# S5 queues re-ordered, and the weights behind each norm converted in a room of their own without GpSimd

## The chip, the core and the metric

The kernel runs on one core of a Trainium2 chip. The engines named here are TensorE (PE), VectorE (DVE), ScalarE (ACT), GpSimd (POOL) and SyncE (SP), each with an instruction queue that it works off in order; DMA transfers are issued from SP's and ACT's queues. The metric is the device time of one execution in microseconds, the median of the runs.

## The reference

One step of a trunk with two layers. Layer 0 mixes with an S5 state space model, layer 1 with an RG-LRU; each is followed by a residual layer norm, a gated FFN with a causal convolution of width 3, and another norm. There are 512 prompt tokens with 16 meta tokens ahead (528 positions) and 8 running sequences of 8 tokens, 592 columns in all; the model is 1024 wide, the FFN 2816.

```python
def _trunk(h, ...):
    for i in range(DEPTH):                       # DEPTH = 2
        if i % N_MIXERS == 0:
            mix, sr, si = s5_mixer(h, ...)       # u = x @ w_in; B u; scan; C s + d u; gelu; GLU @ w_out
        else:
            mix, hr, cb = rglru_mixer(h, ...)    # conv4, gates, linear recurrence, @ w_out
        h = layer_norm(DN_ALPHA * h + mix, ...)
        f, fb = conv_ffn(h, ...)                 # up, conv3, gelu(gate) * value, down
        h = layer_norm(DN_ALPHA * h + f, ...)

def layer_norm(x, g, b):
    mu = jnp.mean(x, -1, keepdims=True)
    var = jnp.mean(jnp.square(x - mu), -1, keepdims=True)
    return (x - mu) * lax.rsqrt(var + LN_EPS) * g + b
```

All of it is computed in float32, and the states and convolution histories are returned with the outputs.

## The kernel before

**Layout and products.** Activations lie transposed: 128 channels on the partitions, the 592 columns along them, eight tiles `RES[0..7]` for the 1024 channels. A product is made in two halves of 296 columns. Each float32 operand is held as a rounded high part and the remainder, and every block of 128 x 128 weights costs three matmuls, in `mm3`:

```python
T.matmul(out, hi[:, k, :], xh, start=start, stop=False)    # L151, hi,whi
T.matmul(out, hi[:, k, :], xl, start=False, stop=False)    # L152, lo,whi
T.matmul(out, lo[:, k, :], xh, start=False, stop=stop)     # L153, hi,wlo
```

**Weights.** `load` fetches a 512 KB tile by SP's queue into one of three raw buffers; `convert_hi` (L122, ACT) makes `whi`, `convert_lo` (L131, DVE, or POOL where the call passes `G`) makes `wlo = raw - whi`, each from a pool of four. `weights` hands the next pair out, in a fixed order of `keys`, and normally converts ahead as it does so.

**Stages.** By the trace: S5 until 204 us, its GLU until about 297, norm 0 until 336, FFN 0 until 741, norm 1 until 779, RG-LRU until 939, norm 2 until 969, FFN 1 until 1372, the last norm and the output until 1401.

**S5.** The order of the work is written by hand (`manual_schedule`): each engine's queue holds its instructions in the order in which the Python calls stand. Ahead of the loop, a generator `ahead` of small operations on the parameters is pumped by `some(n)`, while `split_x` (L295 the low half) and the first projections run. `turn` transposes operators through PSUM (L504, copied at L506), `turn_b` does so for the B operators that `bbar` makes (L414 to L416), `phases` and `tables` (L462 to L479) make the discretised coefficients, `projection(m, h)` multiplies by `w_in` and `projected` copies the result out (L449).

The loop has eight steps s. A step spreads the B operators by a matmul with a selection (`flip_b` L519, `flipped` L525 and L526, giving `bt`; `spread` and `operators` L534 to L542, giving `xw`), makes the state inputs (`states`, L605, 64 matmuls of 74 columns), scans on DVE (`scans`, L618 to L626), turns the states back (`turned`, L634 to L639, giving `sx`), saves the `ends` of the states (L643, L644 on ACT, which read `sx`), and makes the outputs of the step before (`outputs`, L656 from `sx`, L660 from the Toeplitz operator `toe`). `lags`, `windows` and `assemble` (L559, L562, L550 on POOL, L569, L584) build those operators. `gy_hi` and `gy_lo` (L685, L689) split the gelu's output for the GLU, whose first products stand at the end of step 6.

**Norms.** `skewed` overlaps a norm with the last products ahead of it (`tail` of them) and with the first products behind it. Columns 0 to 295 are finished for all tiles first; while the norm works on them, PE makes the other half. A norm sums z and z squared on POOL (L906, L907), totals them over channels by a matmul with ones (L920, L922), makes mean and scale (`centered`, L934 to L955, POOL L940), and applies them tile by tile (`applied`: DVE L973, ACT L974 the high part, DVE L979 the low part). `plan` is a table that says what else is queued at which tile: numbers are the evacuations of tail products, functions are weight conversions. The three first weights behind the norm, `nxt`, are handed out without converting ahead; the plan converts them, seven of the nine low parts in all on POOL.

**FFN.** A pool of its own opens with the FFN; it loads the convolution's history by ACT's queue and scales it on POOL (`hist`, L1138 to L1141). The norm's offsets are added to `RES` by POOL (L1002) at the start; L1161 adds the history and L1166 is the gelu.

## Time and profile before

| | |
|---|---|
| runs | 1402.67, 1402.8, 1412.2 us; median 1402.8 |
| profiled execution | 1403.13 us; span 1401.3 us, mean granted TensorE clock 0.980 |
| PE busy | 1333.1 us (95%) in 10680 matmuls |
| DVE busy | 840.2 us (60%) |
| ACT busy | 582.7 us (42%) |
| POOL busy | 301.1 us (21%) |
| chain that ended last | PE 76%, DVE 17%, ACT 4%, issue 2%, POOL 1% |
| weight conversions on DVE, L131 | 181, mean 1265 ns |

The span is the time from the first to the last instruction on the profiled execution. PE is the engine with the most work, so the places of interest are those where it is not busy: the page's slices show them in the first seventh of the span and in short dips after it. "PEclk" is the clock that TensorE was granted, as a share of 2.4 GHz; the lower of its two levels, 1.2 GHz, reads 0.5. A matmul that waits shows in brackets how long and for which instruction of which engine.

### The profile page before, as it was taken

How to read it: one execution, taken by the hardware profiler on the slowest of the kernel's cores; microseconds unless marked ns; L12 is line 12 of the kernel's file. 1: busy time of each engine (PE TensorE's matmuls, PEld its weight loads, DVE VectorE, ACT ScalarE, POOL GpSimd, SP SyncE). 2: the span in 40 equal slices, each digit the busy share in tenths (PEclk: the TensorE clock that was granted, in tenths of full speed). 3: DMA queues.
4: the chain of work that ended last, by engine and by line, in shares of the span. 5: the costliest groups of instructions: out<-in, count | busy, mean ns of one | idle time of the engine just before them, and what ended most of it. 6: DMA issues, size and time to landing. Idle time of an engine off the chain costs nothing.

```text
span 1401.3 us, 25545 instructions
## 1 busy us (share of the span) xinstructions
PE 1333.1 (95%) x10680; PEld 1308.4 (93%) x10680; DVE 840.2 (60%) x1421; ACT 582.7 (42%) x942; POOL 301.1 (21%) x368
## 2 busy tenths in 40 slices
PE   6979889999999999999998999998999999999995
PEld 6978889988999999999998999998999999999994
DVE  8758936358655255535547889849655245535546
ACT  3645534235343133313433587734444124313433
POOL 1313402247000000000037431167100000000036
PEclk9979979999999999999999999999999999999998
DMA  6525554211322222222221212221322222222211
GB/s 221 162 82 138 132 177 136 76 61 61 106 76 84 83 76 85 67 91 91 66 82 61 93 45 92 96 68 61 107 90 77 90 78 85 74 97 81 77 52 68
DMA packets 72035, 127.65 MB, mean 91 GB/s; under 512 B 21232, under 2 KB 43888, under 8 KB 71920
## 3 DMA queue, kind: packets, MB, share of 16 engines
q1 hardware_dynamic: 62160, 120.45, 27.1%
q10 hardware_dynamic: 9760, 5.57, 1.4%
q8 instruction: 84, 1.38, 0.4%
q14 instruction: 31, 0.25, 0.1%
HBM read 113.35 MB, written 12.66 MB: 90 GB/s over the span
## 4 chain that ended last, share of the span: by engine, by line
PE 76%; DVE 17%; ACT 4%; issue 2%; POOL 1%; DMA 0%; SPq 0%; DVEq 0%; ACTq 0%
PE mm L152 24%; PE mm L153 24%; PE mm L151 24%; DVE wlo L131 2%; DVE res L973 1%; DVE lo L979 1%; PE mm L656 1%; DVE xw L542 1%; DVE res L945 1%; PE mm L660 1%; PE mm L605 1%; DVE t L635 1%; ACT res L479 1%; DVE res L968 1%; ACT whi L122 1%
## 5 line engine op out<-in xcount | busy, mean ns | idle before, releaser
L152 PE MATMUL mm<-lo,whi 128*128 128x296 f32 (+2 forms) x2816 | 843.9, 300 | 17.9 <-DVE lo L979 9.8
L151 PE MATMUL mm<-hi,whi 128*128 128x296 f32 (+2 forms) x2816 | 845.4, 300 | 13.8 <-ACT whi L122 6.8
L153 PE MATMUL mm<-hi,wlo 128*128 128x296 f32 (+2 forms) x2816 | 842.7, 299 | 2.8 <-DVE wlo L131 2.8
L152 PEld LDWEIGHTS mm<-lo,whi 128*128 128x128 f32 x2816 | 535.2, 190 | 23.9 <-DVE lo L979 14.5
L151 PEld LDWEIGHTS mm<-hi,whi 128*128 128x128 f32 x2816 | 535.1, 190 | 16.5 <-ACT whi L122 6.8
L153 PEld LDWEIGHTS mm<-hi,wlo 128*128 128x128 f32 x2816 | 534.7, 190 | 4.0 <-DVE wlo L131 4.0
L131 DVE TENSOR_TENSOR wlo<-wraw,whi 128x1024 fp32r<-128x1024 f32 (+1 forms) x181 | 228.2, 1265 | 220.0 <-ACT whi L122 219.3
L122 ACT ACTIVATE whi<-wraw 128x1024 fp32r<-128x1024 f32 (+1 forms) x188 | 194.5, 1039 | 302.5 <-PE mm L152 297.5
L1161 POOL TENSOR_TENSOR tmp<-tmp,hist 128x16 f32<-128x16 f32 x88 | 20.5, 235 | 697.4 <-DVE tmp L1158 697.4
L1156 DVE SCALAR_TENSOR_TENSOR tmp<-mm,sm,tmp 128x512 f32<-128x512 f32 (+2 forms) x176 | 132.1, 750 | 0.0
L1160 ACT ACTIVATE stg<-mm 128x18 f32<-128x18 f32 x88 | 16.4, 186 | 185.6 <-DVE tmp L1158 185.5
L1208 DVE TENSOR_TENSOR res<-mm,res 128x296 f32<-128x296 f32 (+3 forms) x48 | 26.0, 558 | 80.5 <-PE mm L153 80.5
L1151 ACT ACTIVATE tmp<-mm,sm 128x592 f32<-128x592 f32 (+1 forms) x88 | 72.2, 822 | 0.0
L1167 DVE TENSOR_TENSOR tmp<-tmp 128x592 f32<-128x592 f32 (+1 forms) x44 | 33.8, 767 | 38.7 <-ACT tmp L1166 38.7
L906 POOL TENSOR_TENSOR s<-s,res 128x296 f32<-128x296 f32 (+2 forms) x45 | 41.8, 930 | 60.9 <-DVE res L1114 31.2
L168 DVE TENSOR_TENSOR lo<-tmp,hi 128x592 fp32r<-128x592 f32 (+2 forms) x48 | 36.7, 764 | 29.6 <-ACT hi L167 29.6
L550 POOL TENSOR_TENSOR v<-cq,ap 128x512 f32<-128x512 f32 x32 | 42.5, 1359 | 49.8 <-ACT cq L494 41.1
L167 ACT ACTIVATE hi<-tmp 128x592 fp32r<-128x592 f32 (+2 forms) x48 | 33.1, 690 | 43.9 <-DVE tmp L1167 30.0
L1002 POOL TENSOR_SCALAR res<-res,sm 128x592 f32<-128x592 f32 (+1 forms) x24 | 49.2, 2065 | 6.3 <-DVE lo L979 6.3
L907 POOL TENSOR_TENSOR s<-s,tmp 128x296 f32<-128x296 f32 (+2 forms) x53 | 50.4, 955 | 0.2 <-ACT tmp L902 0.2
L902 ACT ACTIVATE tmp<-res 128x296 f32<-128x296 f32 (+2 forms) x56 | 24.0, 445 | 58.0 <-DVE res L1208 24.7
L1206 DVE SCALAR_TENSOR_TENSOR res<-res,mm 128x592 f32<-128x592 f32 (+1 forms) x16 | 12.2, 762 | 59.2 <-PE mm L153 59.2
(277 smaller groups left out, 1237.4 us busy)
## 6 DMA issues: line engine op xcount, KB each, us to landing
wraw<-in_wup SPq DMA_DIRECT2D x88, 512.0 KB, 3.4
wraw<-in_wdn SPq DMA_DIRECT2D x32, 448.0 KB, 3.3
wraw<-in_w5o SPq DMA_DIRECT2D x16, 512.0 KB, 4.3
wraw<-in_wdn SPq DMA_DIRECT2D x16, 512.0 KB, 3.5
wraw<-in_wri SPq DMA_DIRECT2D x16, 512.0 KB, 3.6
wraw<-in_w5i SPq DMA_DIRECT2D x8, 512.0 KB, 4.4
td<-lagsb SPq DMA_DIRECT2D x8, 512.0 KB, 3.4
lagged<-td SPq DMA_DIRECT2D x8, 512.0 KB, 4.2
```

Source lines behind the costliest of these rows:

```text
L122: A.activation(hi[:, 0:kk, :], t[:, 0:kk, :], AF.Copy)
L131: eng.tensor_tensor(lo[:, 0:kk, :], t[:, 0:kk, :], hi[:, 0:kk, :].bitcast(F32), op=ALU.subtract)
L151: T.matmul(out, hi[:, k, :], xh, start=start, stop=False)
L152: T.matmul(out, hi[:, k, :], xl, start=False, stop=False)
L153: T.matmul(out, lo[:, k, :], xh, start=False, stop=stop)
L168: V.tensor_tensor(lo[:, scols], src[:, scols], hi[:, scols].bitcast(F32), op=ALU.subtract)
L550: G.tensor_tensor(v[:, m], c[:, a, :, :, None].to_broadcast(sh), b[:, NQ * q:NQ * q + NQ, None, 1:CH + 1].to_broadcast(sh), op=ALU.mult)
L906: G.tensor_tensor(self.s1[:, cs_], RES[0][:, cs_] if m == 1 else self.s1[:, cs_], z, op=ALU.add)
L907: G.tensor_tensor(self.s2[:, cs_], self.s2[:, cs_], sq[:, cs_], op=ALU.add)
L1002: G.tensor_scalar(z, z, bm, None, op0=ALU.add)
L1151: A.activation(acc[:, d0:NT], X(d0, NT), AF.Identity, scale=w[2], bias=fcb[:, l, m:m + 1])
L1156: V.scalar_tensor_tensor(acc[:, a:TP], X(a - sh, TP - sh), w[k], acc[:, a:TP], op0=ALU.mult, op1=ALU.add)
```

## The change

Two parts that have nothing to do with each other, and one small move.

*S5's order.* The opening makes 9 and then 6 of the small parameter operations ahead of the first low half of the weights, where it made 24 and one per tile; `projected(1, 1)` comes ahead of the rest of them; the turn of B operators 0 and 1 comes behind `project(3, 0)`, in another PSUM tile. `bbar(5, 8)`, `phases(1)` and `tables(1)` move from step 0 to ahead of the loop. In each step from 2 on, `flipped(s + 1)` comes ahead of `ends(s - 1)`. `projection(7, 0)` and `toeplitz(0)` move from step 1 to the end of step 0. In steps 6 and 7, `gy_lo(s - 3)` comes ahead of `turned(s)`.

*Weights behind a norm.* Where `nxt` is given, `skewed` opens a pool with two buffers each for `whi` and `wlo`. The first two weights behind the norm are converted into it, on ACT and DVE, one behind each of the last two evacuations of the first half. The third is converted in the plan: its high part at "late", its low part behind the last tile of the first half. No conversion behind a norm is done on POOL. The pool closes with the norm, and the FFN's pool opens after it.

*Room.* The RG-LRU's pool is closed ahead of the tiles of norm 2 instead of behind that norm.

```diff
+        def room(i, name):
+            if i in beside:
+                return beside[i].tile([P, 8, P], F32R, tag=f"x{name}", name=name, bufs=2)
+            return wp.tile([P, 8, P], F32R, tag=name, name=name, bufs=4)
...
-                some(24)
+                some(9)
                 for k in range(DM):
                     split_x(k, 0)
                     if k == 0:
                         load(1)
+                        some(6)
                         convert_next()
-                    some(1)
-                    if k == 3:
-                        load(2)
+                    else:
+                        some(1)
+                load(2)
...
+                projected(1, 1)
                 some(200)
-                projected(1, 1)
...
-                turn_b(0, 2)
                 convert_next()
                 project(3, 0)
+                turn_b(0, 2, 1)
+                projected(3, 0)
                 flip_b(0)
-                projected(3, 0)
...
                 bbar(2, 5)
-                assemble(1)
+                phases(1)
+                bbar(5, 8)
                 flip_b(1)
                 flipped(1)
+                assemble(1)
...
                 projection(4, 0)
+                tables(1)
                 turn_b(2, 5)
...
                 for s in range(DM):
                     last = s == DM - 1
+                    if 1 < s < DM - 1:
+                        flipped(s + 1)
                     run(ends, s - 1)
...
-                    if 1 < s < DM - 1:
-                        flipped(s + 1)
...
-                    run(toeplitz, s - 1)
+                    if s > 1:
+                        toeplitz(s - 1)
...
-                    if s == 1:
-                        projection(7, 0)
                     run(outputs, s - 1)
                     run(fetch_gy, s - 2)
+                    if s >= DM - 2:
+                        gy_lo(s - 3)
                     turned(s)
...
                         flipped(2)
-                        phases(1)
-                        tables(1)
                         convert_next()
                         projection(6, 0)
-                        bbar(5, 8)
+                        turn_b(5, 8)
                         phases(2)
                         tables(2)
                         projection(6, 1)
-                        turn_b(5, 8)
                         phases(3)
                         tables(3)
-                    run(gy_lo, s - 3)
+                        projection(7, 0)
+                        toeplitz(0)
+                    if s < DM - 2:
+                        run(gy_lo, s - 3)
...
-            with tc.manual_schedule():
+            with ExitStack() as ex:
+                if nxt:
+                    own = ex.enter_context(tc.tile_pool(name=f"own{norm.i}", bufs=1))
+                    beside.update({keys.index(key): own for key in nxt[:2]})
+                ex.enter_context(tc.manual_schedule())
                 for i, m in enumerate(end):
                     pair(i, 0)
                     prod(m, 0, 0, n, ahead=i < tail // 2)
                     evac(m, 0)
+                    if nxt and i >= tail - 2:
+                        load(at["conv"] + 3)
+                        convert(at["conv"] + 1)
...
-                        {"late": lambda: (A.activation(scr, scr, AF.Tanh), convert_hi(at["conv"] + 2)),
-                         0: [lambda: convert_lo(at["hi"], G)], 1: [0], 3: [1],
-                         5: [lambda: convert(at["conv"] + 1, G)]}, tail=2)
+                        {"late": lambda: (A.activation(scr, scr, AF.Tanh), convert_hi(at["conv"] + 1)),
+                         1: [0], 3: [1], 8: [lambda: convert_lo(at["hi"])]}, tail=2)
...
-        PLAN = {"late": lambda: convert_hi(at["conv"] + 2),
-                0: [lambda: convert_lo(at["conv"] + 1, G), 1, lambda: convert_lo(at["conv"] + 1)],
-                3: [2], 4: [3], 6: [lambda: convert(at["conv"] + 1, G)]}
+        PLAN = {"late": lambda: convert_hi(at["conv"] + 1), 0: [1], 3: [2], 4: [3],
+                8: [lambda: convert_lo(at["hi"])]}
...
+        rgs.close()
         HL3 = hltiles()
         opened = skewed(list(range(3, DM)), ro_prod, ro_evac, norm, gcols, HL3, up_first(1), DM, (4, 6), PLAN, slots)
         nc.sync.dma_start(o_rgc, rgc)
         nc.sync.dma_start(o_rgh, rgh)
-        rgs.close()
```

The lines of the changed kernel stand a few numbers lower: L504 becomes L509, L605 L610, L656 L661, L689 L694, L131 L136, L973 L983, L979 L989, L1208 L1225.

PE's queue in steps 0 and 1, before. L504 turns B operators 5 to 7, L605 is `states(1)`, L656 and L660 are `outputs(0)`; at the dots stand the 24 products of projection (7,0).

```order
L504 MATMUL mm<-ident,bb 128x128 x3
L605 MATMUL mm<-u,xw 64x74 x32
L559 MATMUL mm<-cq,bst_123 32x16 x8
L562 MATMUL mm<-v,bst_123 32x112 x16
L534 MATMUL mm<-aT,sel_126 128x128 x8
...
L656 MATMUL mm<-sx_154,v 128x74 x32
L660 MATMUL mm<-u,toe 128x74 x8
```

The same place with the change; at the dots stand the products of projections (6,1) and (7,0), 48 of them.

```order
L509 MATMUL mm<-ident,bb 128x128 x3
...
L610 MATMUL mm<-u,xw 64x74 x32
L564 MATMUL mm<-cq,bst_123 32x16 x8
L567 MATMUL mm<-v,bst_123 32x112 x16
L539 MATMUL mm<-aT,sel_126 128x128 x8
L661 MATMUL mm<-sx_154,v 128x74 x32
L665 MATMUL mm<-u,toe 128x74 x8
```

The turn comes 24 products earlier, and `outputs(0)` stands directly behind the operators' matmuls (L534, now L539), with projection (7,0) ahead of all of them.

DVE's queue at the end of step 6, before. L626 is the scan, L542 the operators of the next step, L634 to L639 `turned`, L689 `gy_lo(3)`.

```order
L626 SCALAR_TENSOR_TENSOR t<-d_1938,t 128x296 x2
L570 SCALAR_TENSOR_TENSOR lagsb<-diag,sp_107,mm 128x16
L542 TENSOR_TENSOR xw<-bt,mm 128x1024 x2
L634 TENSOR_TENSOR t<-t,res_73 128x592
L635 TENSOR_TENSOR t<-t,res_73 128x592
L638 TENSOR_TENSOR sx_154<-t 128x4x74
L639 TENSOR_TENSOR sx_154<-t 128x4x74
L689 TENSOR_TENSOR lo<-res_70,hi 128x592
L570 SCALAR_TENSOR_TENSOR lagsb<-diag,sp_107,mm 128x16
```

With the change:

```order
L631 SCALAR_TENSOR_TENSOR t<-d_1938,t 128x296 x2
L575 SCALAR_TENSOR_TENSOR lagsb<-diag,sp_107,mm 128x16
L547 TENSOR_TENSOR xw<-bt,mm 128x1024 x2
L694 TENSOR_TENSOR lo<-res_70,hi 128x592
L639 TENSOR_TENSOR t<-t,res_73 128x592
L640 TENSOR_TENSOR t<-t,res_73 128x592
L643 TENSOR_TENSOR sx_154<-t 128x4x74
L644 TENSOR_TENSOR sx_154<-t 128x4x74
L575 SCALAR_TENSOR_TENSOR lagsb<-diag,sp_107,mm 128x16
```

`gy_lo` stands ahead of the four instructions of `turned`, which come one instruction later.

DVE's queue in norm 1, before. L1208 is an evacuation of the FFN's down products, L951 to L955 are the statistics of the first half, L973 applies tile 0 and tile 1; the second weight's low part stands between them.

```order
L951 TENSOR_TENSOR tmp<-tmp 128x296
L945 TENSOR_TENSOR res_69<-res_69,mm 128x296
L953 SCALAR_TENSOR_TENSOR tmp<-tmp 128x296
L945 TENSOR_TENSOR res_70<-res_70,mm 128x296
L955 SCALAR_TENSOR_TENSOR tmp<-tmp 128x296
L973 SCALAR_TENSOR_TENSOR res_67<-res_67,sm,tmp 128x296
L1208 TENSOR_TENSOR res_72<-mm,res_72 128x296
L131 TENSOR_TENSOR wlo<-wraw,whi 128x1024
L973 SCALAR_TENSOR_TENSOR res_68<-res_68,sm,tmp 128x296
L979 SCALAR_TENSOR_TENSOR lo<-res_67,sm,hi 128x296
```

With the change, the last evacuations of the first half, and ahead of the statistics (L944) the two conversions:

```order
L1225 TENSOR_TENSOR res_72<-mm,res_72 128x296
L1225 TENSOR_TENSOR res_73<-mm,res_73 128x296
L136 TENSOR_TENSOR wlo<-wraw,whi 128x1024
L1225 TENSOR_TENSOR res_74<-mm,res_74 128x296
L136 TENSOR_TENSOR wlo<-wraw,whi 128x1024
L944 TENSOR_TENSOR tmp<-mm,tmp 128x296
L945 TENSOR_SCALAR tmp<-tmp 128x296
```

The two low parts stand before the statistics; between the changed kernel's first two L983 only the evacuation L1225 is left, and the third low part comes behind the last L989 of the half.

## Rows read from the trace of the kernel before

**Rows 1.** Windows by stage: bounds, length, busy us by engine, PEclk, DMA share, GB/s.

```profile
36.00:109.00 73.00, 64.63 (x669) 60.38 (x670) 43.66 (x91) 39.74 (x89) 15.95 (x20) 0.88 0.40 122
...
109.00:174.00 65.00, 59.71 (x1112) 53.73 (x1111) 59.33 (x74) 37.16 (x81) 26.08 (x28) 1.00 0.53 137
...
174.00:204.00 30.00, 24.94 (x297) 23.15 (x296) 12.45 (x17) 8.11 (x11) 2.79 (x3) 0.79 0.56 171
...
297.00:336.00 39.00, 33.31 (x204) 30.42 (x202) 34.73 (x54) 19.34 (x36) 26.11 (x20) 0.91 0.12 41
...
336.00:741.00 405.00, 404.99 (x2974) 404.97 (x2974) 204.90 (x313) 139.94 (x210) 37.25 (x68) 1.00 0.26 84
...
741.00:779.00 38.00, 32.21 (x209) 29.19 (x207) 33.19 (x55) 17.64 (x34) 29.59 (x26) 1.00 0.13 42
...
939.00:969.00 30.00, 26.07 (x174) 23.92 (x172) 25.64 (x42) 13.46 (x26) 19.61 (x18) 1.00 0.16 53
```

**Rows 2.** Waits of PE: instruction, what it waited for, total us, times, longest.

```profile
PE mm L559 <- ACT bt L526: 5.3, 3, 3.3
...
PE mm L504 <- DVE ph L462: 4.0, 1, 4.0
```

**Rows 3.** Timeline of VectorE and ScalarE, opening: start, duration, engine, line, operation, tiles, count.

```profile
10.19 1.22 DVE L131 TENSOR_TENSOR wlo<-wraw,whi 128x1024 fp32r<-128x1024 f32 x1
...
36.34 0.29 DVE L416 TENSOR_TENSOR bb<-t 128x128 f32<-128x128 f32 x1
...
37.22 0.38 ACT L506 ACTIVATE bB<-mm 128x256 f32<-128x256 f32 x1 [0.58 <-PE mm L504]
```

**Rows 4.** Timeline of PE, with the wait before an operation in brackets.

```profile
40.35 1.16 PE L519 MATMUL mm<-bB,sel 64*128 64x128 f32 x16
...
78.38 3.85 PE L605 MATMUL mm<-u,xw 128*64 128x74 f32 x64
...
91.82 6.56 PE L656 MATMUL mm<-sx,v 64*128 64x74 f32 x64 [2.40 <-ACT ut L449]
...
98.31 3.69 PE L660 MATMUL mm<-u,toe 128*128 128x74 f32 x16
...
108.82 2.27 PE L605 MATMUL mm<-u,xw 128*64 128x74 f32 x64
...
114.01 3.80 PE L656 MATMUL mm<-sx,v 64*128 64x74 f32 x64
...
117.73 2.01 PE L660 MATMUL mm<-u,toe 128*128 128x74 f32 x16
...
177.80 0.61 PE L152 MATMUL mm<-lo,whi 128*128 128x296 f32 x1 [3.35 <-DVE lo L689]
...
968.61 0.40 PE L151 MATMUL mm<-hi,whi 128*128 128x296 f32 x1 [1.48 <-ACT hi L974]
```

**Rows 5.** Windows in which PE runs only projections, columns as before.

```profile
85.80:89.42 3.62, 3.62 (x28) 3.29 (x24) 3.48 (x7) 3.55 (x14) 0.00 (x0) 1.00 0.00 0
...
101.73:107.22 5.49, 5.49 (x26) 5.24 (x25) 0.00 (x0) 0.73 (x2) 0.99 (x1) 0.60 0.62 134
```

**Rows 6.** Timeline of VectorE, steps 5 and 6.

```profile
164.43 0.78 DVE L618 TENSOR_TENSOR t<-mm,res 128x592 f32<-128x592 f32 x1 [2.35 <-PE mm L605]
...
170.90 0.77 DVE L634 TENSOR_TENSOR t<-t,res 128x592 f32<-128x592 f32 x1
...
175.75 1.99 DVE L689 TENSOR_TENSOR lo<-res,hi 128x592 fp32r<-128x592 f32 x1
```

**Rows 7.** Timelines of GpSimd and VectorE, norm 1.

```profile
750.23 2.61 POOL L131 TENSOR_TENSOR wlo<-wraw,whi 128x1024 fp32r<-128x1024 f32 x1
...
750.89 3.03 DVE L131 TENSOR_TENSOR wlo<-wraw,whi 128x1024 fp32r<-128x1024 f32 x1
```

**Rows 8.** Timeline of GpSimd: the FFN's history work, and the start of FFN 0.

```profile
216.59 0.85 POOL L1138 TENSOR_TENSOR hist<-hist,sm 128x352 f32<-128x352 f32 x1 [3.12 <-DMA hist<-in_fhist]
...
328.87 17.86 POOL L1002 TENSOR_SCALAR res<-res,sm 128x592 f32<-128x592 f32 x8 [2.87 <-DVE lo L979]
```

More of the change, by code (lines that the diff above doesn't have):

```diff
@@ L106, in trunk @@
         keys += ffn_keys(0) + rg_keys() + ffn_keys(1)
-        raw, ready = {}, {}
+        raw, ready, beside = {}, {}, {}
         at = {"load": 0, "hi": 0, "conv": 0, "get": 0}
@@ L120, in convert_hi @@
                 t, kk = raw[at["hi"]]
-                hi = wp.tile([P, 8, P], F32R, tag="whi", name="whi", bufs=4)
+                hi = room(at["hi"], "whi")
                 A.activation(hi[:, 0:kk, :], t[:, 0:kk, :], AF.Copy)
@@ L129, in convert_lo @@
                 hi = ready[at["conv"]][0]
-                lo = wp.tile([P, 8, P], F32R, tag="wlo", name="wlo", bufs=4)
+                lo = room(at["conv"], "wlo")
                 eng.tensor_tensor(lo[:, 0:kk, :], t[:, 0:kk, :], hi[:, 0:kk, :].bitcast(F32), op=ALU.subtract)
@@ L498, in assemble, with turn @@
                 CC[q] = c
-            def turn(dst, srcs):
-                pt = psum(2)
+            def turn(dst, srcs, tile=2):
+                pt = psum(tile)
                 for n, s_ in enumerate(srcs):
@@ L506, in turn, with turn_b @@
                 A.activation(dst, pt[:, 0:n * P].rearrange("p (n s) -> p n s", n=n), AF.Copy)
-            def turn_b(a0, a1):
-                turn(bT[:, a0:a1], [bb[:, q].rearrange("p r i h -> p (r i h)") for q in range(a0, a1)])
+            def turn_b(a0, a1, tile=2):
+                turn(bT[:, a0:a1], [bb[:, q].rearrange("p r i h -> p (r i h)") for q in range(a0, a1)], tile)
             def flip_b(q):
```

## The prediction

> **What bounds the kernel now.** I read the profile by stages first, in the view of windows [rows 1]: at each stretch the reader compares what TensorE (PE) was busy with the length of the stretch, and looks at the granted clock. In the first FFN, 336 to 741 us, PE is busy 404.99 of 405.00 us: nothing that the change does there can shorten it, and something late there costs only what PE cannot cover. What PE loses lies in the S5 stage and around the norms: 36 to 109 us, 64.63 busy of 73 and a clock of 0.88; 109 to 174, 59.71 of 65 at full clock, but with VectorE (DVE) busy 59.33 too; 174 to 204 with a clock of 0.79; and the norms with 33.31 of 39, 32.21 of 38 and 26.07 of 30. Then the list of PE's waits says who ended them [rows 2], and the timelines of PE and DVE, one after the other at the same times, say whether the engine waited for was itself busy [rows 3 to 8]. The last is what decides: a wait of PE for an engine that is never idle does not go away when the order is changed.
>
> The profiled execution took 1403.13 us (span 1401.3), 0.33 above the median of the runs, so a sum against it holds for the median.
>
> **The change, part by part.**
>
> *Opening.* The first weights' low half is converted ahead of the chain of small operators instead of behind it, and the turn of the first two B operators goes behind projection (3,0). Small waits of PE before 37 us go, but the operators need the last `bb`, which DVE writes at 36.34 to 36.63 [rows 3], with the same small operations ahead of it in both orders. Behind it come two transposes and ScalarE's copy, which ends at 37.61 in this trace already [rows 3], so L519 can start at about 37.6 instead of 40.35 [rows 4]: **-2.75**. The bounds are 0 (`bb` later, because a low half of 1.22 us [rows 3] and more now stand ahead of its chain) and -3.7 (nothing behind `bb`).
>
> *Steps 0 and 1 (40 to 109 us).* PE's transposes of the operators 5 to 8 wait 4.0 us for DVE's `ph` [rows 2], because `bbar(5, 8)` stands in step 0 behind the phases and tables of step 1; it now stands ahead of the loop. L656 of step 0 waits 2.40 us for ScalarE's copy of a projection [rows 4]; the order shows that projection (7,0) now comes ahead of L605 and L656 follows that group directly. Both waits go: -6.4. DVE, busy 43.66 of 73, and ScalarE, 39.74 of 73, have room to do the same work earlier [rows 1]. Behind these waits PE ran at the lower of its two levels, 1.2 GHz: the same 64 short matmuls of L605 took 3.85 at 78.38 and 2.27 at 108.82; L656 6.56 and 3.80; L660 3.69 and 2.01 [rows 4]; and products of two projections, 26 in 5.49 us, against 28 in 3.62 where the clock was full [rows 5]. The differences are 1.6 + 2.8 + 1.7 + 1.9 = 8.0. Each of these stretches follows a wait of PE; with the waits gone I count the whole 8.0. Together **-14.4**; the bounds are -6.4 (the level stays) and 0 for what another engine ends instead.
>
> *Steps 2 to 5 (109 to 164 us).* PE's 5.3 us of waits for `bt` [rows 2] come from ScalarE's queue: `bt` stood behind copies that wait for DVE's `sx`, and now stands ahead of them. But DVE has no gap between 111 and 162 us and sets the step, about 13.4 us, where PE needs 59.71/5 = 11.9 [rows 1]. So what goes is only DVE's own idle time, 2.35 us before L618 at 164.43 [rows 6]: **-2.35**, not -5.3. The bounds are 0 and -5.3.
>
> *Step 6.* The low half of the gelu's output (L689) comes ahead of `turned`, as soon as L542 is done: at 170.90, where L634 started, instead of 175.75 [rows 6]. PE waited 3.35 us for it, then ran 14 products at half rate [rows 4], 1.8 us more than by the full-rate row of [rows 5]. So between -3.35 and -5.15; with `lo` 4.85 earlier I take **-4.8**. In step 7 the same exchange removes a PE wait but puts the last `sx` 1.2 us later, and the states' products wait for that instead: 0. From 174 to 204 the clock column says 0.79 [rows 1]: at 0.5 for the lower level that is some 12.6 us at half rate, or 6.3 lost, of which 1.8 are counted above; the other 4.5 may come back, which I keep for the low end.
>
> *Norms 0 to 2.* Seven weight conversions leave GpSimd (POOL) and the first two behind each norm are done in the tail, in tiles of their own. What they cost is seen on DVE in norm 1: beside POOL's conversion, 2.61 us from 750.23, a conversion on DVE takes 3.03 us from 750.89 [rows 7], against 1.22 us of the same operation at 10.19 [rows 3], and the norm's own operations are queued behind it. PE's idle time around the three norms is 39 - 33.31, 38 - 32.21 and 30 - 26.07, 15.4 us in all [rows 1]. The three restarts (0.86, 1.39 and 1.48; the last in [rows 4]) stay: the third conversion, now on DVE, stands ahead of the second half's statistics and takes the place of the slowed operation there. Of the 11.7 that are left I count 10; of the half rate around norm 0 (clock 0.91 over 39 us, 3.5 us lost [rows 1]) I count 2. Together **-12**, between 0 and -17.
>
> Here a rule has to be weighed. The DVE row at 750.89 looks like an operation that stood still: POOL's conversion beside it ended 1.95 us after it began, and 1.95 + 1.22 makes 3.17, close to the 3.03. By the Trainium skill, page "SBUF — State Buffer", section on the two separate sides of SBUF, GpSimd and VectorE share a port pair that one of them holds for a whole instruction; the row agrees. That rule speaks for taking the conversions away, but also says that POOL's sums L906 and L907, about 1 us each in the page's list of groups, still stop a DVE operation each, and these now fall beside L973 and L979; two such per norm at 0.5 us make 3 us, and the sum of the norms -9.
>
> *What is hidden.* With the room of its own the FFN's history load and its four POOL operations come behind the room's release, so behind POOL's eight L1002 (17.86 us); each of the four is like the row at 216.59, 0.85 us [rows 8]. The first gelu waits for that, some 3.5 us longer; PE has about 10 us of products for other accumulators in that time, and shows no gap [rows 1]. Without that cover it would be +3.5 at two FFN starts.
>
> The sum is -2.75 - 14.4 - 2.35 - 4.8 - 12 = -36.3, and 1403.1 - 36.3 = **1367 us**.
>
> **Rivals.**
>
> *The waits of S5 come back elsewhere.* ScalarE and DVE get the same work in less time; if each wait that is removed finds the next one half as long, S5 gives 12 of 24.3: 1379. For it: DVE is continuous in five steps. Against it: both are busy under 60% before 109 us.
>
> *The norms give nothing.* DVE takes over seven conversions of 1.22, 8.5 us, and stops by L906 and L907 on the path add 3 (two a norm at 0.5); together they use up the 12: 1379. For it: DVE is busy 34.73 of 39 around norm 0 [rows 1]. Against it: two of three conversions lie in a tail where DVE waits for PE.
>
> *The change does not do what it says.* The conversions in the tail need raw weights that have landed, with three buffers for them. If they come late, ScalarE and DVE stand before the norm's own chain for about one landing, 3.4 us a norm by the page's list of DMA issues, so the norms turn from -12 to +10: 1389.
>
> *Slower.* In steps 2 to 7 PE does nothing but short matmuls, and these ran at the lower level in steps 0 and 1. If the denser order falls to that level and stays there until 204 us, a step's 11.9 us of PE become 20.8 by the three pairs in [rows 4] (14.1 for 8.1), against DVE's 13.4: +7.4 a step, five steps +37; the 8.0 counted above do not come back, and 174 to 204 goes from 0.79 to 0.5, +10: 1367 + 37 + 8 + 10 = 1422. With the +8 and +10 it is above the old time from three such steps on. Against it: at 109 to 174 the clock was 1.00 with waits of 3.3 us in it [rows 1, 2]; fewer waits should not lower it.
>
> **How the numbers follow.** Forecast 0.66, waits come back in S5 0.13, norms give nothing 0.12, late weights 0.05, slower 0.04. The time is the forecast's, 1367. The range: down to 1354, if the 4.5 us of clock in steps 6 and 7, the 5 us by which the norms fall short of their bound, and some 3 us of steps 2 to 5 come as well; up to 1386, which takes in the first two rivals with the 3.5 us of history work at both FFN starts. About one in five lies outside. A difference of 1%, 14 us, is what a measurement of this kernel can tell from no change. Below 1389 lie the forecast and the first two rivals but for their tails, and half of the third: faster 0.88; within 1% 0.08; slower 0.04.
>
> **What would show it.** In the changed profile: L519's counterpart near 37.5 us; no PE wait over 1 us between 40 and 95; the same three groups of short matmuls near 2.3, 3.8 and 2.0 us from step 0 on; DVE without a gap through steps 2 to 6; no wait for `lo` in step 6; the S5 stage some 24 us shorter; no weight conversion on POOL, and no L955, L973 or conversion on DVE above 1.3 us around the norms; FFN windows with PE busy to the last tenth. Wrong if the half-rate rows stay, if the norms' PE idle time stays above 12 us, or if the first gelu of an FFN stops PE.

## The result

The changed kernel takes 1367.12 us in the median of four runs (1364.53 to 1367.29), against 1402.81 before: a ratio of 0.9725, 95% interval 0.9684 to 0.9767. In a second set of runs the same two kernels stood at 1363.98 and 1403.38 (0.9713, 0.968 to 0.9746). The profiled execution is the fastest of the first four, 1364.53 us with a span of 1362.4, so in the two profiles 38.9 us of span have gone, some 3 more than in the medians.

Where they went is read from the starts of the same work on PE in both profiles. "Lead" is how much earlier the changed kernel starts it; the gain of a stretch is the difference of two leads:

| work on PE | before | after | lead | gained in the stretch | predicted |
|---|---|---|---|---|---|
| first spreading of B operators (L519, L524) | 40.35 | 36.61 | 3.74 | 3.74 | 2.75 |
| states of step 2 (L605, L610) | 108.82 | 90.46 | 18.36 | 14.62 | 14.4 |
| states of step 6 | 162.11 | 139.18 | 22.93 | 4.57 | 2.35 |
| states of step 7 | 183.32 | 156.93 | 26.39 | 3.46 | 4.8 |
| the GLU behind S5's outputs | 203.76 | 177.84 | 25.92 | -0.47 | 0 |
| end of the GLU, start of norm 0 | 298.35 | 271.70 | 26.65 | 0.73 | 0 |
| last products of FFN 0 | 742.16 | 711.36 | 30.80 | 4.15 | norms: 12 in all |
| RG-LRU's first products | 771.32 | 736.89 | 34.43 | 3.63 | |
| RG-LRU's last products | 939.85 | 905.41 | 34.44 | 0.01 | 0 |
| FFN 1's first products | 968.61 | 930.47 | 38.14 | 3.70 | |
| end of the span | 1401.3 | 1362.4 | 38.9 | 0.76 | |

PE's list of waits of the changed kernel, whole program: total, times, longest.

```profile
PE mm L156 <- ACT whi L127: 6.8, 1, 6.8
...
PE mm L661 <- ACT sx L649: 2.0, 2, 1.6
```

The waits for `bt` and for `ph` [rows 2] are not in it. The first line is the wait for the first weights and stands in both kernels.

The timeline of PE, changed kernel, the rows that answer to [rows 4]:

```profile
36.61 1.16 PE L524 MATMUL mm<-bB,sel 64*128 64x128 f32 x16 [0.52 <-issue]
...
74.16 2.27 PE L610 MATMUL mm<-u,xw 128*64 128x74 f32 x64
...
79.81 3.80 PE L661 MATMUL mm<-sx,v 64*128 64x74 f32 x64 [0.40 <-ACT sx L649]
83.54 2.01 PE L665 MATMUL mm<-u,toe 128*128 128x74 f32 x16
...
90.46 2.27 PE L610 MATMUL mm<-u,xw 128*64 128x74 f32 x64
...
152.95 0.40 PE L157 MATMUL mm<-lo,whi 128*128 128x296 f32 x1 [1.31 <-DVE lo L694]
...
167.37 7.11 PE L661 MATMUL mm<-sx,v 64*128 64x74 f32 x64 [1.63 <-ACT sx L649]
174.41 3.69 PE L665 MATMUL mm<-u,toe 128*128 128x74 f32 x16
...
930.47 0.40 PE L156 MATMUL mm<-hi,whi 128*128 128x296 f32 x1 [1.15 <-ACT hi L984]
```

In steps 0 and 1 the short matmuls run at the full rate, 2.27, 3.80 and 2.01 us. In step 6 a wait for `lo` is left, 1.31 us where it was 3.35, without half rate behind it. In step 7 the short matmuls still run at half rate, 7.11 and 3.69 us, here behind a wait of 1.63 us for `sx`; in the kernel before they took 6.38 and 3.69, six products behind a wait of 1.71 us for `lo`.

Windows between the same starts, columns of [rows 1]. First steps 0 and 1, the kernel before and the changed one, and steps 2 to 5 of the changed one:

```profile
40.35:108.82 68.47, 60.88 (x640) 56.77 (x639) 41.41 (x84) 37.75 (x85) 15.95 (x20) 0.88 0.42 125
```

```profile
36.61:90.46 53.85, 52.74 (x638) 48.99 (x638) 49.42 (x88) 36.98 (x83) 17.38 (x20) 1.00 0.52 153
90.46:139.18 48.72, 48.03 (x898) 42.79 (x896) 45.49 (x57) 31.47 (x73) 18.82 (x22) 1.00 0.58 147
```

In steps 0 and 1 PE's idle time fell from 7.59 to 1.11 us, by 6.5, and its busy time for the same work from 60.88 to 52.74, by 8.1, with the clock column up from 0.88 to 1.00.

Then norm 0 with FFN 0, norm 1, and norm 2, the kernel before and the changed one:

```profile
298.35:742.16 443.81, 438.11 (x3177) 435.18 (x3175) 239.64 (x367) 159.46 (x244) 63.81 (x87) 0.99 0.25 80
742.16:771.32 29.16, 24.02 (x157) 21.82 (x155) 25.68 (x42) 12.27 (x26) 21.26 (x21) 1.00 0.16 55
...
939.85:968.61 28.76, 24.84 (x168) 23.03 (x166) 25.25 (x42) 12.22 (x26) 18.76 (x17) 1.00 0.17 56
```

```profile
271.70:711.36 439.66, 434.83 (x3177) 432.82 (x3175) 236.82 (x370) 158.81 (x246) 62.53 (x88) 1.00 0.26 81
711.36:736.89 25.53, 23.24 (x157) 21.73 (x155) 23.69 (x43) 11.25 (x24) 15.38 (x19) 1.00 0.17 54
...
905.41:930.47 25.06, 23.91 (x168) 22.89 (x167) 23.08 (x43) 11.17 (x25) 13.04 (x15) 1.00 0.15 56
```

Idle time fell from 5.70, 5.14 and 3.92 us to 4.83, 2.29 and 1.15, by 6.5 in all; the other 5.0 of the 11.5 gained here are PE's busy time, 3.3 of them in the first window. There half rate has gone: the 39 us from 270.35 on read 1.00 in the clock column, where [rows 1] had 0.91. In the other two windows the column says 1.00 in both kernels, and what makes up their 1.7 us is not told apart.

The timeline of VectorE in norm 1, the place of [rows 7]:

```profile
718.80 0.97 DVE L983 SCALAR_TENSOR_TENSOR res<-res,sm,tmp 128x296 f32<-128x296 f32 x1
...
720.07 0.51 DVE L983 SCALAR_TENSOR_TENSOR res<-res,sm,tmp 128x296 f32<-128x296 f32 x1
720.51 1.09 DVE L989 SCALAR_TENSOR_TENSOR lo<-res,sm,hi 128x296 fp32r<-128x296 f32 x1
721.52 1.08 DVE L983 SCALAR_TENSOR_TENSOR res<-res,sm,tmp 128x296 f32<-128x296 f32 x1
...
724.65 1.08 DVE L989 SCALAR_TENSOR_TENSOR lo<-res,sm,hi 128x296 fp32r<-128x296 f32 x1
```

The second tile is applied 1.27 us behind the first. Before, the conversion of 3.03 us [rows 7] stood between them. What is still slow, 1.09, 1.08 and 1.08 instead of 0.51, lies beside GpSimd's sums, the first two beside these (timeline of GpSimd):

```profile
720.29 0.98 POOL L916 TENSOR_TENSOR s<-s,res 128x296 f32<-128x296 f32 x1 [0.84 <-DVE res L1225]
721.23 1.05 POOL L917 TENSOR_TENSOR s<-s,tmp 128x296 f32<-128x296 f32 x1
```

### The profile page after: what moved, and what is told of

The parts are those of the page before. It is cut to its first block, busy times and chain, and to the rows that moved or that the text cites. A ratio compares the mean times of both kernels' runs of the same rounds, so it can differ in the third digit from the quotient of the medians.

```text
span 1362.4 us, 25545 instructions
## 1 busy us (share of the span) xinstructions
PE 1316.4 (97%) x10680; PEld 1293.7 (95%) x10680; DVE 840.4 (62%) x1428; ACT 581.5 (43%) x942; POOL 289.0 (21%) x361
## 4 chain that ended last, share of the span: by engine, by line
PE 73%; DVE 20%; issue 3%; ACT 3%; POOL 1%; DMA 0%; SPq 0%; DVEq 0%; ACTq 0%
PE mm L158 23%; PE mm L157 23%; PE mm L156 23%; DVE wlo L136 2%; DVE res L983 2%; DVE lo L989 1%; DVE xw L547 1%; DVE ph L471 1%; PE mm L661 1%; DVE res L955 1%; DVE t L640 1%; DVE tmp L1355 1%; DVE ini L1352 1%; DVE t L639 1%; POOL s L917 0%
## 5 line engine op out<-in xcount | busy, mean ns | idle before, releaser
L156 PE MATMUL mm<-hi,whi 128*128 128x296 f32 (+2 forms) x2816 | 841.8, 299 | 11.7 <-ACT whi L127 6.8
L136 DVE TENSOR_TENSOR wlo<-wraw,whi 128x1024 fp32r<-128x1024 f32 (+1 forms) x188 | 233.1, 1245 | 207.7 <-ACT whi L127 207.0
L1225 DVE TENSOR_TENSOR res<-mm,res 128x296 f32<-128x296 f32 (+3 forms) x48 | 25.9, 558 | 78.9 <-PE mm L158 78.8
L1012 POOL TENSOR_SCALAR res<-res,sm 128x592 f32<-128x592 f32 (+1 forms) x24 | 54.5, 2288 | 6.2 <-DVE lo L989 6.2
L555 POOL TENSOR_TENSOR v<-cq,ap 128x512 f32<-128x512 f32 x32 | 43.2, 1381 | 38.9 <-DVE ph L471 37.1
```

What stands on the lines that cost most here:

```text
L136: eng.tensor_tensor(lo[:, 0:kk, :], t[:, 0:kk, :], hi[:, 0:kk, :].bitcast(F32), op=ALU.subtract)
L555: G.tensor_tensor(v[:, m], c[:, a, :, :, None].to_broadcast(sh), b[:, NQ * q:NQ * q + NQ, None, 1:CH + 1].to_broadcast(sh), op=ALU.mult)
L1012: G.tensor_scalar(z, z, bm, None, op0=ALU.add)
```

## The experiments

Times are medians; the kernel before, beside them, took 1403.3, 1403.4 and 1403.1 us in the three sets.

### Do the two parts add up?

`s5_only` puts the norms' part back, the plans of all three norms and the early end of the RG-LRU's pool with it (cut):

```diff
-            with ExitStack() as ex:
-                if nxt:
-                    own = ex.enter_context(tc.tile_pool(name=f"own{norm.i}", bufs=1))
+            with tc.manual_schedule():
...
+                        {"late": lambda: (A.activation(scr, scr, AF.Tanh), convert_hi(at["conv"] + 2)),
+                         0: [lambda: convert_lo(at["hi"], G)], 1: [0], 3: [1],
+                         5: [lambda: convert(at["conv"] + 1, G)]}, tail=2)
```

> The re-ordered S5 queues with the weights behind the norms converted as before (seven low parts on GpSimd, no room of their own). Theory: the two parts add up; by the two profiles the S5 stage ends 26.6 us earlier, so 1402.8 - 26.6 = 1376.2, with the S5 stretch as in the changed kernel and the norms as in the one before. Rival: part of the norms' gain came from the new S5 order (where the norm falls against the weight loads), then the time lies clearly below 1374; or part of S5's gain needs the other part, then above 1380.

Measured: 1376.87 us (1375.2 to 1382.1), ratio 0.982 (0.9795 to 0.9845). S5 alone gives 26.5 us.

`norm_only` is the kernel before with the room and the plan of the change, and S5 in the old order.

> The weights behind the norms in a room of their own and none on GpSimd, with the S5 order as before. Theory (parts add up): the norms give 4.2 + 3.7 + 4.1 = 12.0 us by the two profiles, so 1402.8 - 12 = 1390.8. Rival: the norms gain only because the engines arrive less loaded out of S5; then norm 0 gives nothing here and the time is 1395 or more.

Measured: 1392.24 us (1391.82 to 1400.58), ratio 0.9933 (0.991 to 0.9956): 11.1 us. The sum of the two is 37.6 us; the changed kernel gave 35.7 in its first set and 39.4 in the second. The parts add up as closely as these sets agree with one another.

### Waits and half rate in steps 0 and 1

`steps01` does one piece on the kernel before (cut):

```diff
                 bbar(2, 5)
-                assemble(1)
+                phases(1)
+                bbar(5, 8)
                 flip_b(1)
                 flipped(1)
+                assemble(1)
...
+                tables(1)
                 turn_b(2, 5)
...
-                    if s == 1:
-                        projection(7, 0)
...
+                        projection(7, 0)
+                        toeplitz(0)
```

> Only one piece of the S5 change on the kernel before: the B operators 5 to 8 and phases and tables of step 1 ahead of the loop, projection (7,0) and the Toeplitz operator of step 0 at the end of step 0. Theory (the half rate follows PE's waits and goes with them): 6.4 us of waits and 8.0 us of half rate go, 1402.8 - 14.4 = 1388.4, with L605, L656 and L660 of steps 0 and 1 at 2.3, 3.8 and 2.0 us. Rival (the clock is a matter of the stage, not of these waits): the waits go and the half rate stays, 1396.4, with L656 still above 6 us.

Measured: 1389.82 us (1388.74 to 1390.74), ratio 0.9903 (0.9888 to 0.9917): 13.5 us. Its PE timeline in steps 1 and 0:

```profile
78.94 2.27 PE L605 MATMUL mm<-u,xw 128*64 128x74 f32 x64
...
84.54 3.80 PE L656 MATMUL mm<-sx,v 64*128 64x74 f32 x64 [0.35 <-ACT sx L644]
88.27 2.01 PE L660 MATMUL mm<-u,toe 128*128 128x74 f32 x16
```

The same matmuls took 3.85, 6.56 and 3.69 [rows 4]. Its window from the first spreading of B operators to the states of step 2:

```profile
41.88:95.17 53.29, 52.44 (x639) 48.94 (x638) 48.83 (x84) 37.91 (x85) 18.02 (x20) 1.00 0.53 154
```

Beside the 68.47 us of the kernel before these are 15.2 less, 6.7 of idle time and 8.4 of busy time; 1.5 of it is spent ahead of the window, which begins at 41.88 instead of 40.35. So more than half of the gain is the rate of the work behind the waits. The rival, 1396.4, is out.

### Steps 2 to 6: which engine sets the step

`flip_behind` undoes the move of `flipped` in the changed kernel, `gy_behind` that of `gy_lo`; `after_again` is the changed kernel beside them.

```diff
-                    if 1 < s < DM - 1:
-                        flipped(s + 1)
                     run(ends, s - 1)
...
                     load(min(at["conv"] + 3, 12))
+                    if 1 < s < DM - 1:
+                        flipped(s + 1)
```

```diff
-                    if s >= DM - 2:
-                        gy_lo(s - 3)
                     turned(s)
...
-                    if s < DM - 2:
-                        run(gy_lo, s - 3)
+                    run(gy_lo, s - 3)
```

> The changed kernel as it is, beside the next three on the same chip: 1367 (1364.5 to 1367.3 so far).

> The changed kernel with one piece undone: in steps 2 to 6 the copies that give bt stand behind the saved ends of the states again. The prediction took 2.35 us for this piece, because VectorE had no gap in these steps and would set them at 13.4 us in either order; the profiles show 4.6 us and steps of 12.2. Theory A (PE's wait for bt sets the step, and VectorE's 13.4 were stretched by what GpSimd does beside it): +4.6, 1371.7, VectorE's step back at about 13.3 us. Theory B (VectorE's work sets the step, and the gain came from the work moved out of the loop): +2 or less, 1367 to 1369.

> The changed kernel with one piece undone: in steps 6 and 7 the low half of the gelu's output comes behind the turned states again. By the two profiles this piece gave 3.5 us in step 6 and nothing in step 7. Theory: +3.5, 1370.6, with a PE wait of some 3 us for lo in step 6. Rival: the half rate that PE shows in step 7 in both kernels depends on it, then +5 to +8, or, if it goes with the other order, 0.

Measured: 1363.98 us for the changed kernel (1363.28 to 1365.98), 1368.64 (1367.29 to 1369.57) and 1373.32 (1371.68 to 1375.13): +4.7 and +9.3. The intervals of the ratios touch (0.9707 to 0.9785 and 0.9743 to 0.9811 beside 0.968 to 0.9746); the ranges of the runs don't.

The +4.7 is the difference that theory A gave, and VectorE's step is 13.6 us on average, near A's 13.3; but A's reason, VectorE's work stretched by GpSimd, is not what the rows show. The same three waits of PE are back in `flip_behind`, by its list of waits from 90.5 to 145 us:

```profile
PE mm L564 <- ACT bt L531: 5.3, 3, 3.3
```

VectorE waits for PE twice behind them, 0.76 us in front of L547 and 1.75 us at step 6 (`flip_behind`, timeline of VectorE):

```profile
147.34 0.78 DVE L623 TENSOR_TENSOR t<-mm,res 128x592 f32<-128x592 f32 x1 [1.75 <-PE mm L610]
```

That makes 2.5 us, near the 2.35 that the prediction took. From step 2's scan to step 6's VectorE is busy 51.02 of 54.48 us here and 51.70 of 52.64 in `after_again`: its work is not longer, it waits. The profiles do not show the rest of the +4.7. The profiled execution of `flip_behind`, the fastest of its four, is only 1.3 us above that of `after_again`, the slowest of its four, so where the rest lies stays open.

What PE's waits were worth in the change itself, VectorE's rows say. The first operation of the scan, L618, in steps 2 and 7, kernel before (step 6 is in [rows 6]):

```profile
111.14 0.77 DVE L618 TENSOR_TENSOR t<-mm,res 128x592 f32<-128x592 f32 x1 [17.03 <-PE mm L605]
...
185.64 0.78 DVE L618 TENSOR_TENSOR t<-mm,res 128x592 f32<-128x592 f32 x1 [1.66 <-PE mm L605]
```

and in steps 2, 6 and 7 of the changed kernel:

```profile
92.78 0.78 DVE L623 TENSOR_TENSOR t<-mm,res 128x592 f32<-128x592 f32 x1 [2.50 <-PE mm L610]
...
144.56 0.78 DVE L623 TENSOR_TENSOR t<-mm,res 128x592 f32<-128x592 f32 x1
...
159.25 0.77 DVE L623 TENSOR_TENSOR t<-mm,res 128x592 f32<-128x592 f32 x1 [1.32 <-PE mm L610]
```

From step 2 to step 6 VectorE took 53.29 us before, 2.35 of them a wait for PE, and 51.78 after: it gained 1.5, where PE gained 4.57. PE ran ahead of VectorE, which lags by 3 us at 144.56, where no wait is shown. PE's lead is spent in step 6: from there to step 7 VectorE gained 21.21 - 14.69 = 6.5 us, PE 3.46. In that step VectorE had not been the limit before, busy 13.31 of the 21.21 us. Whether the two pieces have prices of their own stays open: undone one by one they cost 4.7 and 9.3 us in the medians, 14.0 where both together gave 8.0, but by the start of norm 0 in the profiles, against `after_again`, only 1.35 and 6.3. Without `gy_lo`'s move, PE in step 6 waits 5.04 us for VectorE instead of the 3.35 of [rows 4] (`gy_behind`, timeline of PE):

```profile
158.87 0.62 PE L157 MATMUL mm<-lo,whi 128*128 128x296 f32 x1 [5.04 <-DVE lo L694]
```

and the half rate that this row begins (0.62 us) lasts for 11 of the 13 products behind it. In its profile norm 0 begins 6.3 us later than in that of `after_again`, 278.5 against 272.2, of which this wait against the 0.39 us there is 4.65. The +9.3 lies beyond the rival's +8, but the two profiled executions are only 7.2 us apart, as that of `after_again` is 2.0 above its median. So the profiles account for about 7 us, and not for the rest.

### Norms: the place or the engine

`plan_dve` has the new S5 order and the old places of the conversions, all on VectorE. Against `s5_only`, norm 0 (the plan of norms 1 and 2 is changed likewise):

```diff
-                         0: [lambda: convert_lo(at["hi"], G)], 1: [0], 3: [1],
-                         5: [lambda: convert(at["conv"] + 1, G)]}, tail=2)
+                         0: [lambda: convert_lo(at["hi"])], 1: [0], 3: [1],
+                         5: [lambda: convert(at["conv"] + 1)]}, tail=2)
```

> The new S5 order, and the weights behind the norms converted at the places of the kernel before and in the shared room, but all low parts on VectorE instead of seven of them on GpSimd. Theory of the place (the gain comes from conversions that no longer stand in the norm's own chain): VectorE then has up to three of 1.22 us in the chain in place of operations slowed by GpSimd, so about as the S5 order alone: 1374 to 1378. Theory of the engine (the gain comes from GpSimd not holding VectorE up): nearly the whole of the norms' 12 us stays, 1365 to 1368.

Measured: 1375.19 us (1374.99 to 1377.3), 1.7 below `s5_only`. Timeline of VectorE in norm 0:

```profile
279.79 0.53 DVE L983 SCALAR_TENSOR_TENSOR res<-res,sm,tmp 128x296 f32<-128x296 f32 x1
280.23 2.36 DVE L136 TENSOR_TENSOR wlo<-wraw,whi 128x1024 fp32r<-128x1024 f32 x2
282.50 0.52 DVE L983 SCALAR_TENSOR_TENSOR res<-res,sm,tmp 128x296 f32<-128x296 f32 x1
```

Each conversion takes 1.2 us now, but both stand between the first two tiles. At the old places the engine alone is worth 1.7 of about 11 us, and the runs of the two kernels overlap, so it may be worth nothing there.

`room_pool` does the reverse on the changed kernel: the place stays, the engine goes back.

```diff
-                        convert(at["conv"] + 1)
+                        convert(at["conv"] + 1, G)
```

> The changed kernel with one edit: the two low parts converted in the tail, in the room of their own, are made by GpSimd (2.4 to 2.6 us each) instead of VectorE (1.2). The third stays on VectorE. Theory of the place, which the run with all conversions on VectorE at the old places spoke for: the tail has room for them on GpSimd too, within 3 us of the changed kernel, 1364 to 1368. Theory of the engine: they are stretched and stretch VectorE's evacuations, and GpSimd's sums of the norm come late; 4 us or more, 1369 and up.

Measured: 1369.07 us (1368.63 to 1370.91), 2.0 above the changed kernel's first set and 5.1 above its second. The median lies at the low end of what the theory of the engine gave, 1369 and up, and one us above the theory of the place. In the profiles PE takes 2.1 us more than in the changed kernel from norm 0 to norm 1, 2.1 from norm 1 to norm 2 and 0.1 behind it. GpSimd's conversions in the tail take 2.36 to 2.41 us. In norms 1 and 2 the last sums of the norm stand behind one of them, and PE waits 1.94 and 0.57 us for these; PE's list, whole program, has

```profile
PE mm L930 <- POOL s L916: 3.3, 3, 1.9
```

in place of 1.3 us in two waits. So of the norms' 11 to 12 us the room and the place give some 7, with two of three conversions still on GpSimd. The engine gives the other 4 by these profiles, more at the new place, where GpSimd has the norm's sums to make, than at the old.

### The work that was counted at nothing

`hist_more` repeats one of the four history operations eight times:

```diff
             G.tensor_tensor(th, hist[:, :, :, 1], w1b, op=ALU.mult)
+            for _ in range(8):
+                G.tensor_tensor(th, hist[:, :, :, 1], w1b, op=ALU.mult)
```

> The changed kernel with the FFN's history work made longer: one of its four GpSimd operations (0.85 us) repeated eight more times, +6.8 us on GpSimd at the start of each FFN. The prediction counted the 3.5 us of that work at nothing, because PE has about 10 us of products for other accumulators there. If that cover is as counted, 6.5 us are left and the time moves by less than 1 us: 1364 to 1368. If the cover is already used up, +6.8 at each of two FFNs: 1378 to 1381.

Measured: 1364.91 us (1363.46 to 1366.7), between the medians of the changed kernel in its two sets: no change that these runs can tell, and the rival, 1378 to 1381, is out. ScalarE's wait for the first gelu, in the kernel before, the changed kernel and then in `hist_more`:

```profile
347.13 0.70 ACT L1166 ACTIVATE tmp<-tmp 128x592 f32<-128x592 f32 x1 [3.35 <-POOL tmp L1161]
```

```profile
320.31 0.70 ACT L1183 ACTIVATE tmp<-tmp 128x592 f32<-128x592 f32 x1 [6.94 <-POOL tmp L1178]
```

```profile
328.00 0.70 ACT L1185 ACTIVATE tmp<-tmp 128x592 f32<-128x592 f32 x1 [11.27 <-POOL tmp L1180]
```

It grew from 3.35 us in the kernel before to 6.94, and to 11.27 here, and PE showed no wait over 0.52 us behind the restart of the FFN.

### The end of S5

PE's two last waits and the half rate in step 7 looked like 8 us to be had. `fill` puts ready products of the GLU into them:

```diff
                     if s == 6:
                         GL[0, 0] = psum(0), 0
+                        glu_part(0, 0, 3, False)
                         glu_part(0, 0, 4, False)
...
                 glu_part(0, 0, 5, False)
+                GL[0, 1] = psum(1), 0
+                glu_part(0, 1, 4, False)
                 gy_hi(a - 1)
```

> The changed kernel with PE's two last waits of S5 filled by products of the GLU that are ready: in step 6 the first three input tiles of both halves of the weights come ahead of the fourth, and 24 products of the other half of the columns come ahead of the outputs of step 7. The changed kernel waits 1.31 and 1.63 us there, and then runs L661 and L665 in 7.1 and 3.7 us instead of 3.8 and 2.0. Theory (the half rate follows the waits): -2.9 and -5.0, 1359. Rival (the waits are filled, the half rate stays): -2.9, 1364. Third: PE's new products make the outputs of step 7, and with them the last gelu, late: 1366 or more.

Measured: 1365.68 us (1363.48 to 1366.12), where the changed kernel beside it took 1363.98: no gain. The waits are filled and step 7 runs at full rate, and PE stops a little later instead. Timeline of PE, `fill`:

```profile
168.47 3.80 PE L661 MATMUL mm<-sx,v 64*128 64x74 f32 x64
172.19 2.01 PE L665 MATMUL mm<-u,toe 128*128 128x74 f32 x16
...
198.11 0.58 PE L156 MATMUL mm<-hi,whi 128*128 128x296 f32 x1 [5.08 <-DVE tmp L1133]
```

The changed kernel itself did that in its second profile (`after_again`, PE and then VectorE):

```profile
168.77 3.80 PE L661 MATMUL mm<-sx,v 64*128 64x74 f32 x64 [1.65 <-ACT sx L649]
172.50 2.01 PE L665 MATMUL mm<-u,toe 128*128 128x74 f32 x16
...
200.45 0.59 PE L156 MATMUL mm<-hi,whi 128*128 128x296 f32 x1 [3.81 <-DVE tmp L1131]
```

```profile
190.57 0.17 DVE L1261 TENSOR_SCALAR al<-sm 128x8 f32<-128x8 f32 x1
...
199.84 0.83 DVE L1131 SCALAR_TENSOR_TENSOR tmp<-tmp,mm 128x296 f32<-128x296 f32 x2
```

From L1261 to L1131 VectorE makes the parameters of the RG-LRU, 9.3 us of small operations, one table change of ScalarE among them, and the GLU's first evacuation stands behind them. In the first profile of the changed kernel, with half rate in step 7 and no wait of PE, this evacuation starts at 199.62, in the second, with full rate, at 199.84. So it is the end of S5 when PE comes early; half rate in step 7 only fills the time until then. `rgp` moves this work, in a pool of its own, to where VectorE is idle, and `fill_rgp` does both:

```diff
                 fetch_gy(b)
                 gy_lo(a)
+                rg_parameters()
                 GL[1, 1] = psum(3), 0
```

> The changed kernel, with the RG-LRU's parameter work (some 40 small operations of VectorE with one table change of ScalarE, 9 us from first to last) queued ahead of the last gelu's split in S5 instead of behind it. In the profiles in which S5 ran without the half rate at its end, PE waits 3.8 to 5.1 us at about 200 us for the first evacuation of the GLU, which stands behind this work in VectorE's queue. Theory (this work is the end of S5 that the half rate hides): where the half rate comes PE is late anyway and nothing changes; where it doesn't, -3.8; so the median 1361 to 1364 and the lowest at 1360. Rival (the wait is for the data of the last step, not for this work): 1364 to 1367, the wait still there under another name.

> Both edits together: PE's last two waits of S5 filled with ready products of the GLU, and the RG-LRU's parameter work out of the way of its first evacuation. The fill alone gave 1365.7 where the changed kernel beside it gave 1364.0, with PE's waits in steps 6 and 7 gone and a wait of 5.1 us at 198 us in their place. Theory: with that wait gone the 2.9 us of filled waits and most of the half rate are gained at last, 1359. Rival: another end of S5 takes over (weights of the GLU or the residual's load), 1363 or more.

Measured: `rgp` 1367.06 us (1365.11 to 1368.0), above both ranges: the theory's gain did not come, nor the rival's wait. The wait at 200 us is gone, but in its profile PE waits 1.65 us for `sx` and 1.06 for `toe` in step 7, with some half rate behind the second, and norm 0 started at 270.5 us, where the changed kernel's two profiles have 270.9 and 272.2. Another 2.1 us are lost in FFN 1, as the last section says. Half rate in the outputs of step 3 (L691, the changed kernel's L665, 3.7 us) came in both kernels with this edit, so it does not tell them apart. `fill_rgp` took 1360.95 (1359.17 to 1361.73), ratio 0.9697 (0.9683 to 0.9712): it beats both kernels, 42 us below the kernel before. Its PE waits from 140 to 215 us:

```profile
PE mm L156 <- ACT whi L127: 0.7, 1, 0.7
PE mm L158 <- DVE wlo L136: 0.7, 1, 0.7
```

Two edits that gave nothing alone gave 3 to 6 us together, by the set of the changed kernel that they are held against: `fill` alone leaves the wait of 5.08 us for the evacuation, `rgp` alone the waits of step 7, and with both PE has neither. Norm 0 starts at 265.8 us.

## Why the prediction held

The time was forecast at 1367 and came out at 1367.12. That it agrees so closely is luck: the second set gave 39.4 us where 36.3 were summed, and single terms are off by about 1 us, or are right in sum and not in their parts. Point by point:

- **Opening**: 2.75 predicted, 3.74 by PE's starts. The mechanism held, the size was short: I took `bb` as fixed at 36.63, and the chain of small operations ahead of it came 1.04 us earlier (L421 starts at 35.30, L416 at 36.34 [rows 3]). VectorE's own wait of 0.5 us for `whi` has gone from its list; the rest is not taken apart, and no run tried the opening by itself.
- **Steps 0 and 1**: 14.4 predicted, 14.62 measured, 13.5 alone. The parts held too, 6.4 of waits and 8.0 of half rate predicted, 6.5 of idle time and 8.1 of busy time measured. (The 1.9 us for the projections compare 26 products at half rate with 28 at full rate; with 26 in both it is 2.1.) That half rate goes with the waits was the assumption that carried most, and `steps01` shows it.
- **Steps 2 to 6**: 7.15 predicted, 8.03 measured, divided otherwise than I said, 4.57 and 3.46 by PE, 1.5 and 6.5 by VectorE. That VectorE sets the time from step 2 to step 6 was right, and so was not taking the 5.3 us of `bt` waits. The split into 2.35 and 4.8 holds on neither engine, since PE's lead in one step is used in the next. The sign "no wait for `lo` in step 6" failed: 1.31 us of it are left.
- **Step 7**: 0 predicted, -0.47. The wait for `lo` was replaced by one for `sx`, 1.63 us, as written. The 4.5 us of half rate that the low end of the range allowed for did not come back, and would have given nothing: where it did, in `after_again` and `fill`, PE waited 3.81 and 5.08 us behind the RG-LRU's parameters, which I had not looked at.
- **Norms**: 12 predicted, 4.15 + 3.63 + 3.70 and the 0.76 at the end in the profiles, 11.1 by `norm_only`. The sum held, its parts did not: I counted 10 of idle time and 2 of half rate, and measured are 6.5 of idle time and 5.0 of busy time, 3.3 of these around norm 0. The low bound of -17 does not follow from its rows, which give 11.7 of idle time and 3.5 of half rate, 15.2. I counted nothing for the restarts, and they stayed: 1.49, 0.99 and 1.15 us. A new small loss is in the 4.15: PE waits 0.59 us for GpSimd's sums at the start of norm 1. The sign "no conversion on DVE above 1.3 us" failed in the tail of norm 1, 1.59 and 1.41 us. The stops by GpSimd's sums that the Trainium skill (page "SBUF — State Buffer", section on the two separate sides) let me expect are there in norm 1. I had priced two a norm at 0.5 us; its first half alone has three, 1.09, 1.08 and 1.08 against 0.51 us. But the kernel before had three there too, 1.08, 1.07 and 1.08, so they are no new loss; the sum by rows, 12, was nearer than the 9 by that rule.
- **Hidden work**: the history's 3.5 us cost nothing that shows, and neither did 6.8 more.

Of the rivals, waits that come back elsewhere were half right in one place, the end of S5. None of the others happened. The norms gave 11.1 us by themselves; ScalarE's list of waits around the norms has none for a raw weight; and steps 0 to 5 ran at 1.00 in the clock column.

## What to carry to other kernels

A wait of PE can have two prices, its own length and the rate of what follows, and the second can be the larger, as in steps 0 and 1. Where two engines take turns at setting a step, cost a stretch by the one that has no gap, over all steps together. Before counting on a wait's end, look at what stands next in the queues that would then be late: an edit without effect may be the half of a pair. A sum that comes out right should still be checked by its parts, between the same starts in both profiles.

## What was not expected of the hardware

- The same wait need not have the same result. In two executions of the changed kernel PE waited 1.63 and 1.65 us for `sx` in step 7; in one the 64 matmuls behind it took 7.11 us, in the other 3.80.
- The two kernels with the `rgp` edit lose 2.1 us in FFN 1, which the edit does not touch. From the last products of the RG-LRU to those of FFN 1 the profiles of `rgp` and `fill_rgp` take 430.1 us, those of the changed kernel (twice), `fill`, `hist_more` and `room_pool` 427.9 to 428.0. The windows of the changed kernel and of `rgp`:

```profile
905.41:1333.37 427.96, 426.12 (x3195) 424.25 (x3193) 232.35 (x369) 154.61 (x242) 62.42 (x91) 1.00 0.25 80
```

```profile
905.25:1335.34 430.09, 428.24 (x3194) 426.35 (x3193) 233.12 (x369) 154.60 (x242) 62.36 (x91) 1.00 0.25 79
```

The waits of PE are alike and the clock column says 1.00 for both, so its matmuls follow each other a little slower. What in the edit does it stays open.
